# Hybrid encoder trunk on one core: sample attention in a software pipeline, other order of the first tiles and of the last projection, and the merged blocks of the third branch split one block later

## The chip, the cores and the metric

The kernel runs on 1 core of one Trainium2 chip. A core has five engines with one instruction queue each: TensorE (PE, its weight loads PEld), VectorE (DVE), ScalarE (ACT), GpSimd (POOL) and SyncE (SP), which here issues all large DMAs. Each engine executes its queue in order. The metric is device time in microseconds (us), the median of several runs.

## The reference, cut to what matters

One layer on a prompt of 2048 rows and on 8 samples of 16 rows, all with 1024 channels:

```python
h = rms_norm(x, norm_g[l])
(a_x, a_b, a_c, a_z, g_q, g_f, g_i, g_z,
 s_q, s_k, s_v, s_z, m_a, m_b, m_c) = split_cols(h @ w_in[l])
# A: o_a = a_b * conv3(a_c * a_x) * silu(a_z)
# B: o_b = rms_norm(hgrn recurrence(g_q, g_f, g_i)) * silu(g_z)
# C: o_sb = stick-breaking attention(rms_norm(s_q), rms_norm(s_k), s_v) * silu(s_z)
# merged = sigmoid(m_a) * (o_a @ w_branch[0:512]) + sigmoid(m_b) * (o_b @ w_branch[512:1024])
#          + sigmoid(m_c) * (o_c @ w_branch[1024:1536])
# y = x + merged @ w_out
```

Stick-breaking attention of one head, with `z = q @ k.T / 8`: the weight of key j is `sigmoid(z_j)` times the product of `1 - sigmoid(z_i)` over all later visible keys i. The prompt attends to itself, 128 queries at a time. Each of the 8 samples attends with its 16 queries to 1024 cached keys and its own 16. Outputs are y, the conv and recurrence states and the new K and V rows.

## The kernel before, in words

**Tiles and phases.** The 2176 rows form 17 tiles of 128 (tile 0 holds the 8 samples, tiles 1 to 16 the prompt). Phase 1 treats them in three groups (tiles 0 to 4, 5 to 10, 11 to 16), each in chunks of 2 or 3 tiles; phase 2, the merge, in four groups of 5, 4, 4 and 4 tiles (`PGROUPS`, L41).

**Split operands.** Every operand of the big products is split in a high part (ACT copy, L176) and a low part (DVE subtraction, L177): `hh, hl` of the normed rows, `whi, wlo` of the weights, `mh, ml` of the merged rows. A product is three matmuls per 128 rows of contraction: high by high, low by high, high by low.

**Phase 1.** A tile of x is loaded, squared (ACT, L505), scaled by its reciprocal root on POOL (L197) and by `g_bc` on DVE (L510), turned with 8 transposes on PE (L521) and split. Projection jobs follow: `proj_chan` (L587, channels on the partitions, 128x384 or 128x256) and `proj_tok` (L598, tokens on the partitions). Weights come through `wload` (L185, SP) one job ahead. `post_qk` (L682 to 703) norms q and k, turns them (L700) into the tile `kt` (ACT, L702; one buffer) and writes `kt` to DRAM (L703). Gates, conv and recurrence results go to DRAM tensors too.

**Background.** Attention is written as generators that yield costs; `Background` (L58) advances them by a credit that each step of the main work earns. Sample attention runs beside the projections of the second group (about 600 to 1260 us), prompt attention (`attn_pair`, L257 to 328) beside the third group and the merge. The order of instructions on each engine is then fixed by the build, which places each one by its own readiness there.

**Sample attention before** (L344 on). For each sample b and each batch of up to 3 key blocks (`sg` 2, 1, 0): load and turn the key blocks (L405, ACT copy L406), four score matmuls `z` of 32 columns each, one per pair of heads (L412), sigmoids, the scan and the weights `sp` (DVE, L426), three transposes of `sp` (L429, the own keys with 16 columns), copy to `at_` (L436), and then block by block: load `vc` (L444, SP) and four matmuls `pv` (L447) that use 32 columns of the array each.

**Merge** (`merge_jobs`, L1180). For each group, branch x (0 to 2) and pair of blocks dp, `bjob` does for each 128 output channels d: load the gate, 12 matmuls (L1225), multiply with the gate (DVE, L1231 for x = 0, L1233 otherwise), add to `mp` on POOL (L1234) for x > 0, and for x = 2 the split of `mp` into `mh` and `ml` at once. `ojob` (s = 0 to 3) then projects the group's tiles with 256 columns of w_out: 24 matmuls over k = 0 to 7 for each tile (L1247), the sum with x in `yt` (DVE, L1253; one buffer) and its DMA (L1254). The four `ojob`s of a group are written between the first `bjob`s of the next; those of the last group come last.

Of the kernel before, what the change touches and what calls it, by code (L numbers as in the profile page):

```python
# [16 lines left out]
P = 128  # L17
# [81 lines left out]
def trunk(ctx: ExitStack, tc: tile.TileContext, x_prompt, x_sample, cache_conv, state_hgrn, cache_k, cache_v,  # L99
# [72 lines left out]
    nc.sync.dma_start(g_bc, norm_g[0].partition_broadcast(P))  # L172

    def split(hi, lo, src, eng=None):

        nc.scalar.copy(hi, src)  # L176
        (eng or nc.vector).tensor_tensor(lo, src, hi.bitcast(F32), ALU.subtract)  # L177

    def wload(pieces):

        out = []
        for v in pieces:
            a, b = v.shape[1], v.shape[2]
            st = wp.tile([P, a, b], F32, tag="wst", name="wst", bufs=2)
            nc.sync.dma_start(st, v)  # L185
            hi = wp.tile([P, a, b], F32R, tag="whi", name="whi")
            lo = wp.tile([P, a, b], F32R, tag="wlo", name="wlo")
            split(hi, lo, st)
            out.append((hi, lo))
        return out  # L190

    def rstd_of(ssq, n, count):

        v = small.tile([P, n], F32, tag=f"rv{n}", name="rv")
        nc.gpsimd.tensor_scalar(v, ssq, 1.0 / count, EPS, ALU.mult, ALU.add)
        r = small.tile([P, n], F32, tag=f"rr{n}", name="rr")
        nc.gpsimd.tensor_tensor(r, v, mhalf.broadcast_to([P, n]), ALU.pow)  # L197
        return r
# [58 lines left out]
    def attn_pair(m0, m1):  # L257
# [15 lines left out]
        for m in range(m0, m1):  # L273
# [8 lines left out]
            for i in range(nq):  # L282
# [17 lines left out]
                if b0 > 0:  # L300
                    carry[e][i] = at.tile([P, 1], F32, tag="carry", name="carry", bufs=16)
# [42 lines left out]
    def sample_attention():  # L344
# [45 lines left out]
        for b in range(NB):  # L390
            pv = ps_pv()
            carry = one
            vnew = sa.tile([TS, 8, 64], F32, tag="vnew", name="vnew", bufs=1)
            nc.sync.dma_start(vnew, VV[b * TS:(b + 1) * TS])
            for sg in (2, 1, 0):
                nblk = 2 if sg == 2 else 3
                w = nblk * P + (TS if sg == 2 else 0)
                kt = sa.tile([P, 4, 384], F32, tag="kt", name="kt", bufs=2)
                for bi in range(nblk):
                    blk = 3 * sg + bi  # L400
                    kc = sa.tile([P, 512], F32, tag="cst", name="kc", bufs=3)
                    nc.sync.dma_start(kc, cache_k[0, b, blk * P:(blk + 1) * P].rearrange("t h d -> t (h d)"))
                    tp = ps_tp()
                    for h in range(4):
                        nc.tensor.transpose(tp[:, h * P:(h + 1) * P], kc[:, h * P:(h + 1) * P], idf)  # L405
                    nc.scalar.copy(kt[:, :, bi * P:(bi + 1) * P], tp.rearrange("p (h t) -> p h t", h=4))  # L406
                    yield 1.3
                z = ps_z()
                if sg == 2:
                    nc.tensor.matmul(z[:, 256:256 + TS], idb, nmask, start=True, stop=False, skip_group_check=True)  # L410
                for h in range(4):
                    nc.tensor.matmul(z[32 * h:32 * h + 32, :nblk * P], qz[:, h, b], kt[:, h, :nblk * P],  # L412
                                     start=sg != 2, stop=True, skip_group_check=True)
                if sg == 2:
                    for h in range(4):
                        nc.tensor.matmul(z[32 * h:32 * h + 32, 256:256 + TS], qz[:, h, b],
                                         knew[:, h, b * TS:(b + 1) * TS], start=False, stop=True,
                                         skip_group_check=True)
                nc.scalar.activation(sn[:, 384 - w:384], z[:, :w], AF.Sigmoid, scale=-0.125)
                sp = sa.tile([P, 384], F32, tag="sp", name="sp")  # L420
                nc.scalar.activation(sp[:, :w], z[:, :w], AF.Sigmoid, scale=0.125)
                pr = sa.tile([P, 385], F32, tag="pr", name="pr")
                s_in = sn[:, 384 - w:385][:, ::-1]
                nc.vector.tensor_tensor_scan(pr[:, 384 - w:385][:, ::-1], s_in, s_in, carry, ALU.mult, ALU.bypass)
                carry = pr[:, 384 - w:385 - w]
                nc.vector.tensor_tensor(sp[:, :w], sp[:, :w], pr[:, 385 - w:385], ALU.mult)  # L426
                tp = ps_tp()
                for bi in range(nblk):
                    nc.tensor.transpose(tp[:, bi * P:(bi + 1) * P], sp[:, bi * P:(bi + 1) * P], idf)  # L429
                at_ = sa.tile([P, 384], F32, tag="at", name="at_")  # L430
                if sg == 2:
                    nc.tensor.transpose(tp[0:TS, 256:384], sp[:, 256:256 + TS], idf)
                    nc.scalar.copy(at_[:, 0:256], tp[:, 0:256])
                    nc.scalar.copy(at_[0:TS, 256:384], tp[0:TS, 256:384])
                else:
                    nc.scalar.copy(at_, tp[:, :384])  # L436
                yield 2.0
                for bi in range(3):
                    blk = 3 * sg + bi
                    if blk == 8:  # L440
                        vc, n = vnew, TS
                    else:
                        vc, n = sa.tile([P, 8, 64], F32, tag="vst", name="vc", bufs=3), P
                        nc.sync.dma_start(vc, cache_v[0, b, blk * P:(blk + 1) * P])  # L444
                    for h in range(4):
                        c = bi * P + 32 * h
                        nc.tensor.matmul(pv[32 * h:32 * h + 32, 0:P].rearrange("p (e d) -> p e d", e=2),  # L447
                                         at_[0:n, c:c + 32], vc[0:n, 2 * h:2 * h + 2],
                                         start=sg == 2 and bi == 0, stop=sg == 0 and bi == 2, skip_group_check=True)
                    yield 0.6  # L450
            od = sa.tile([P, P], F32, tag="od", name="od", bufs=1)
            nc.scalar.copy(od, pv[:, 0:P])
            for h in range(8):
                nc.sync.dma_start(OCS[b * TS:(b + 1) * TS, h * 64:(h + 1) * 64],
                                  od[h * TS:(h + 1) * TS, 64 * (h % 2):64 * (h % 2) + 64])
            yield 1.0
# [24 lines left out]
    class Prepare:  # L481
# [30 lines left out]
        def turn(self, i, kk):  # L512
# [10 lines left out]
            split(hh[sl], hl[sl], tp.rearrange("p (k t) -> p k t", k=4))  # L523
# [20 lines left out]
        def first_steps(self):  # L544

            n = len(self.tiles)
            for i in range(n):
                self.fetch(i, xp.tile([P, D], F32, tag="xt", name="xt") if i < 2 else
                           g0p.tile([P, D], F32, tag="xt0", name="xt0", bufs=3))
            for f in (self.square, self.scale):  # L550
# [3 lines left out]
            for i in range(n):  # L554
                if i > 2:
                    self.square(i)
                    yield
                    self.scale(i)
                    yield
                for kk in range(0, KB, 4):  # L560
                    self.turn(i, kk)
                    yield
                    if i == 0:
                        (self.scale if kk else self.square)(2)
                self.ready = i

# [74 lines left out]
    lmax = const.tile([P, 4], F32, name="lmax")  # L641
    nc.vector.tensor_copy(lmax, vec[:, 12:16])
    lexp = const.tile([P, 4], F32, name="lexp")
    nc.vector.tensor_tensor(lexp, vec[:, 12:16], lmax, ALU.subtract)
    ebase = const.tile([P, 1], F32, name="ebase")
    nc.vector.memset(ebase, 2.718281828459045)
    nc.gpsimd.tensor_tensor(lexp, ebase.broadcast_to([P, 4]), lexp, ALU.pow)
    lsum = const.tile([P, 4], F32, name="lsum")
    nc.vector.reciprocal(lsum, lexp)
    lsm = const.tile([P, 4], F32, name="lsm")  # L650
    nc.vector.tensor_tensor(lsm, lexp, lsum, ALU.mult)
    lb = const.tile([P, 4], F32, name="lb")
    nc.vector.tensor_tensor(lb, lsm, lsm, ALU.subtract)
    omlb = const.tile([P, 4], F32, name="omlb")
    nc.vector.tensor_scalar(omlb, lb, -1.0, 1.0, ALU.mult, ALU.add)
# [4 lines left out]
    for h in (1, 2, 4, 8, 16, 32, 64):  # L660
        nblk = 64 // h
        mt = g0p.tile([P, 2, 64], F32, tag="mtmp", name="mtmp", bufs=2)
        nc.gpsimd.memset(mt[:, :, :nblk], 1.0)
        for i in range(2):
            m = mt[:, i, :nblk]
            nc.gpsimd.affine_select(m, m, pattern=[[-2 * h, nblk]], base=-h * i, channel_multiplier=1,
                                    compare_op=ALU.is_ge, fill=0.0)
            nc.gpsimd.affine_select(m, m, pattern=[[2 * h, nblk]], base=h + h * i, channel_multiplier=-1,
                                    compare_op=ALU.is_gt, fill=0.0)
        lmask[h] = const.tile([P, 2 * nblk], I32, name=f"lmask{h}")  # L670
        nc.vector.tensor_copy(lmask[h].rearrange("p (i b) -> p i b", i=2), mt[:, :, :nblk])
# [632 lines left out]
```

## Time and profile before

| what | value |
|---|---|
| median of 3 runs | 3031.82 us (3031.12 to 3034.32) |
| the profiled execution's own time | 3036.76 us |
| its span in the trace | 3035.1 us, 51813 instructions |

The span is what the trace covers; 1.7 us of the profiled execution lie around it. Durations and idle times are in us unless ns stands with them. "PE a <- DVE b: 11.0, 21, 2.3" says that PE stood idle 11.0 us in total, 21 times, at most 2.3, ahead of line a until DVE had done line b. In a timeline a row has its start, its duration and, in brackets, the idle time ahead of it and what ended that. PEclk is the clock that TensorE was granted, as a share of full speed. Busy times of single matmuls overlap, since their ends are modelled; the distance of their starts tells their rate.

### The profile page before, as it was taken

The numbers are of one execution on the slowest core, as the hardware profiler recorded it, in microseconds if no ns is written. First come the engines' busy times: TensorE is split into PE (matmuls) and PEld (weight loads), VectorE is DVE, ScalarE is ACT, GpSimd is POOL, SyncE is SP. The second block draws the span as 40 slices with busy tenths as digits, with TensorE's granted clock in tenths as the row PEclk, the third lists the DMA queues.
The fourth block names the chain that finished last, engine by engine and source line by source line (L and its number), as shares of the span: only waits on it lengthen the run. The fifth ranks groups of instructions, "written<-read, shape, count | busy, mean of one in ns | idle before, by whom it ended". The sixth has DMA issues, their size and how long they took to land. (4 is left out here: it accounts for less than half of the span.)

```text
span 3035.1 us, 51813 instructions
## 1 busy us (share of the span) xinstructions
PE 2934.7 (97%) x19609; PEld 2688.3 (89%) x19609; DVE 1759.2 (58%) x3412; ACT 1230.2 (41%) x2571; POOL 454.7 (15%) x861
## 2 busy tenths in 40 slices
PE   7999999999999999999999999999999899899998
PEld 7999999988988888999899998998998788687887
DVE  5345535652434352636635757567577877978753
ACT  4332232243333333224434444444445555555531
POOL 3110000110100000001322111111012412313211
PEclk9999999999999999999999999999999999999999
DMA  5433323455444444323444232323226455555553
GB/s 178 139 109 112 99 90 105 120 161 166 130 126 138 130 131 121 115 78 114 150 152 127 81 122 81 119 66 100 89 87 216 149 164 171 157 184 170 171 160 121
DMA packets 448842, 394.40 MB, mean 130 GB/s; under 512 B 24809, under 2 KB 388674, under 8 KB 448594
## 3 DMA queue, kind: packets, MB, share of 16 engines
q1 hardware_dynamic: 448594, 391.09, 42.3%
q8 instruction: 155, 2.54, 0.4%
q14 instruction: 93, 0.76, 0.1%
HBM read 303.67 MB, written 87.33 MB: 129 GB/s over the span
## 5 line engine op out<-in xcount | busy, mean ns | idle before, releaser
L587 PE MATMUL acc<-hh,whi 128*128 128x384 f32 (+1 forms) x2688 | 937.8, 349 | 0.5 <-ACT hh L176 0.3
L587 PE MATMUL acc<-hl,whi 128*128 128x384 f32 (+1 forms) x2688 | 887.6, 330 | 0.0
L587 PE MATMUL acc<-hh,wlo 128*128 128x384 f32 (+1 forms) x2688 | 887.5, 330 | 0.0
L177 DVE TENSOR_TENSOR wlo<-wst,whi 128x1024 fp32r<-128x1024 f32 x296 | 372.1, 1260 | 435.0 <-ACT whi L176 420.7
L587 PEld LDWEIGHTS acc<-hh,whi 128*128 128x128 f32 x2688 | 508.1, 189 | 37.3 <-issue 31.1
L587 PEld LDWEIGHTS acc<-hl,whi 128*128 128x128 f32 x2688 | 509.2, 189 | 4.9 <-issue 1.0
L587 PEld LDWEIGHTS acc<-hh,wlo 128*128 128x128 f32 x2688 | 507.3, 189 | 0.0
L176 ACT CAST whi<-wst 128x1024 fp32r<-128x1024 f32 x296 | 311.0, 1051 | 364.1 <-PE acc L587 272.4
L598 PE MATMUL acc<-whi,hh 128*128 128x256 f32 x1088 | 317.2, 292 | 7.2 <-DVE gm L986 5.0
L598 PE MATMUL acc<-wlo,hh 128*128 128x256 f32 x1088 | 308.6, 284 | 0.5 <-DVE wlo L177 0.5
L598 PE MATMUL acc<-whi,hl 128*128 128x256 f32 x1088 | 308.6, 284 | 0.0
L298 DVE TENSOR_TENSOR_SCAN pr<-snb,carry 128x513 f32<-128x513 f32 x192 | 259.4, 1352 | 74.3 <-ACT snb L289 73.2
L271 ACT COPY aT<-tp 128x512 f32<-128x512 f32 (+2 forms) x320 | 167.8, 525 | 236.3 <-PE tp L270 233.6
L303 DVE TENSOR_TENSOR sp<-sp,pr 128x512 f32<-128x512 f32 (+2 forms) x320 | 202.0, 631 | 35.1 <-POOL sp L294 13.2
L598 PEld LDWEIGHTS acc<-whi,hh 128*128 128x128 f32 x1088 | 207.2, 190 | 11.7 <-DVE gm L986 5.7
L289 ACT ACTIVATE snb<-z 128x512 f32<-128x512 f32 (+2 forms) x320 | 172.3, 539 | 90.2 <-PE z L286 85.5
L598 PEld LDWEIGHTS acc<-wlo,hh 128*128 128x128 f32 x1088 | 207.4, 191 | 0.7 <-DVE wlo L177 0.7
L598 PEld LDWEIGHTS acc<-whi,hl 128*128 128x128 f32 x1088 | 207.4, 191 | 0.4
L270 PE MATMUL tp<-idf,sp 128*128 128x128 f32 x1088 | 173.1, 275 | 15.8 <-ACT aT L271 15.1
L1225 PE MATMUL acc<-oh,whi 128*128 128x512 f32 (+2 forms) x480 | 179.8, 376 | 8.6 <-DVE gate L1233 7.1
L298 DVE TENSOR_TENSOR_SCAN pr<-snb,one 128x129 f32<-128x129 f32 (+3 forms) x128 | 114.5, 894 | 112.1 <-POOL snb L294 112.0
L291 ACT ACTIVATE sp<-z 128x512 f32<-128x512 f32 (+2 forms) x320 | 171.7, 537 | 16.9 <-DMA OX<-ot 13.0
(301 smaller groups left out, 4773.4 us busy)
## 6 DMA issues: line engine op xcount, KB each, us to landing
wst<-in_w_in_dram SPq DMA_DIRECT2D x216, 512.0 KB, 3.9
wst<-in_w_branch_dram SPq DMA_DIRECT2D x48, 512.0 KB, 4.0
GM<-gm SPq DMA_DIRECT2D x120, 192.0 KB, 2.0
Kt<-KT SPq DMA_DIRECT2D x80, 256.0 KB, 3.1
gate<-GM SPq DMA_DIRECT2D x72, 256.0 KB, 2.7
kc<-in_cache_k_dram SPq DMA_DIRECT2D x64, 256.0 KB, 2.9
vc<-in_cache_v_dram SPq DMA_DIRECT2D x64, 256.0 KB, 2.8
wst<-in_w_out_dram SPq DMA_DIRECT2D x32, 512.0 KB, 4.5
```

The lines of the kernel that those rows point to most:

```text
L176: nc.scalar.copy(hi, src)
L177: (eng or nc.vector).tensor_tensor(lo, src, hi.bitcast(F32), ALU.subtract)
L270: nc.tensor.transpose(tp[:, j * P:(j + 1) * P], sp[:, j * P:(j + 1) * P], idf)
L271: nc.scalar.copy(aT[:, e, 0:nb, i * P:(i + 1) * P], tp[:, :w].rearrange("p (b q) -> p b q", q=P))
L289: nc.scalar.activation(sn[:, 512 - w:512], z[:, :w], AF.Sigmoid, scale=-0.125)
L291: nc.scalar.activation(sp[:, :w], z[:, :w], AF.Sigmoid, scale=0.125)
L298: nc.vector.tensor_tensor_scan(pr[:, 512 - w:513][:, ::-1], s_in, s_in, one if diag else carry[e][i], ALU.mult, ALU.bypass)
L303: nc.vector.tensor_tensor(sp[:, :w], sp[:, :w], pr[:, 513 - w:513], ALU.mult)
L587: nc.tensor.matmul(acc[:, :n], w[0][a][:, k], hT[b][:, k, :n], start=k == 0 and i == 0, stop=k == KB - 1 and i == 2)
L598: nc.tensor.matmul(acc[:, :256], hT[b][:, k, ti * P:(ti + 1) * P], w[k // 4][a][:, k % 4], start=k == 0 and i == 0, stop=k == KB - 1 and i ...
L1225: nc.tensor.matmul(acc[:, :n], w[0][a][:, k, dd * P:(dd + 1) * P], box[x][b][:, k, sl], start=k == 0 and i == 0, stop=k == 3 and i == 2)
```

## The change

What it does, part by part (lines in brackets are of the kernel before):

1. **Start.** The first tile of x is loaded ahead of `g_bc`. Squares and scales of tiles 3 and 4 are held behind the first weight split, the scale of tile 2 behind the split of tile 0 (`tc.issue_after`). The recurrence's bound, the masks and the selectors of the samples (POOL memsets and selects, small DVE copies) are built with the second job.
2. **`post_qk`.** `kt` gets two buffers.
3. **Sample attention** is written as a pipeline over the 24 batches m: keys of m+1, transposes of m, and then the values of m (12 matmuls) directly followed by the scores of m+1. V blocks are loaded three at a time. The own keys are padded with zeros to 128.
4. **Prompt attention.** `carry` has 9 buffers instead of 16.
5. **Merge.** In the third branch the split of a block is written one block later; in the last group it is written at once as before, and there the addition is on DVE. In the first `ojob` of the last group three tiles at a time go through k = 0 to 5 and then through k = 6 and 7. `xr` has 3 buffers (2), `yt` 2 (1).

```diff
 (first_steps)
                 self.fetch(i, xp.tile([P, D], F32, tag="xt", name="xt") if i < 2 else
                            g0p.tile([P, D], F32, tag="xt0", name="xt0", bufs=3))
+                if i == 0:
+                    nc.sync.dma_start(g_bc, norm_g[0].partition_broadcast(P))
...
                 if i > 2:
-                    self.square(i)
-                    yield
-                    self.scale(i)
-                    yield
+                    with tc.issue_after(first_split[0].ins), tc.issue_after(first_split[1].ins):
+                        self.square(i)
+                        yield
+                        self.scale(i)
+                        yield
...
-                    if i == 0:
-                        (self.scale if kk else self.square)(2)
+                    if i == 0 and not kk:
+                        self.square(2)
+                if i == 0:
+                    with tc.issue_after(self.last[1].ins):
+                        self.scale(2)
 (post_qk)
-        kt = qk.tile([P, 4, P], F32R, tag="kt", name="kt", bufs=1)
+        kt = qk.tile([P, 4, P], F32R, tag="kt", name="kt", bufs=2)
 (sample_attention)
+        sps = [single([P, 384], F32, f"sps{i}") for i in range(2)]
+        for x in sps:
+            nc.gpsimd.memset(x, 0.0)
...
+        def turned(m):
...
+            for bi in range(3):
+                nc.tensor.transpose(tp[:, bi * P:(bi + 1) * P], sp[:, bi * P:(bi + 1) * P], idf)
+            at_ = sa.tile([P, 384], F32, tag="at", name="at_")
+            nc.scalar.copy(at_, tp[:, :384])
+            for bi in range(blocks(m)):
+                blk = 3 * sg + bi
+                vc = sa.tile([P, 8, 64], F32, tag="vst", name="vc", bufs=3)
+                nc.sync.dma_start(vc, cache_v[0, b, blk * P:(blk + 1) * P])
...
+        for m in range(last + 1):
+            if m < last:
+                yield from keys(m + 1)
+            turned(m)
+            yield 2.0
+            z = masked(m + 1) if m < last else None
+            values(m)
+            if z is not None:
+                scores(m + 1, z)
+            yield 2.2
 (bjob)
-                            nc.gpsimd.tensor_tensor(m, m, gate[:, sl], ALU.add)
+                            (nc.vector if final and x == 2 else nc.gpsimd).tensor_tensor(
+                                m, m, gate[:, sl], ALU.add)
                         if x == 2:
-                            split(box["h"][:, d, sl], box["l"][:, d, sl], m)
+                            box["due"].append((box["h"][:, d, sl], box["l"][:, d, sl], m))
+                            while len(box["due"]) > (0 if final or d == 7 and chunk is pg[-1] else len(pg)):
+                                split(*box["due"].pop(0))
 (ojob)
+            cuts = [KB - 2, KB] if final and s == 0 else [KB]
...
+                    for c, end in enumerate(cuts):
+                        for ti in some:
...
+                            for k in range(cuts[c - 1] if c else 0, end):
```

The order on PE in the middle of the sample attention, beside a projection with 384 columns (`pv` are the values of one batch, `z` the scores of the next). Before:

```order
L587 MATMUL acc<-hh,wlo 128x384
L447 MATMUL pv<-vc,at__11137 32x128 x4
L587 MATMUL acc<-hh,whi 128x384
L587 MATMUL acc<-hl,whi 128x384
L587 MATMUL acc<-hh,wlo 128x384
L587 MATMUL acc<-hh,whi 128x384
L587 MATMUL acc<-hl,whi 128x384
L587 MATMUL acc<-hh,wlo 128x384
L447 MATMUL pv<-vc,at__11137 32x128 x4
```

Now, with the same projection at L648:

```order
L648 MATMUL acc<-hh,wlo 128x384
L484 MATMUL pv<-vc,at__11236 32x128 x12
L438 MATMUL z<-kt,qz 32x384 x4
L648 MATMUL acc<-hh,whi 128x384
L648 MATMUL acc<-hl,whi 128x384
```

The three groups of four value matmuls stand together, and the scores of the next batch stand right behind them. Over the whole kernel the groups of matmuls on 32 columns that stand apart from each other go from 105 to 33, of which the sample attention has 96 before and 25 now; 8 groups of transposes of 16 columns go as well.

The order on DVE in the third branch of the third merge group, where attention runs beside it (`gate` is the gate product of a block, `ml` the low part of a merged block; `pr` and `sp` belong to attention). Before:

```order
L177 TENSOR_TENSOR ml<-mp,mh 128x512
L303 TENSOR_TENSOR sp<-sp,pr 128x384
L298 SCALAR_TENSOR_TENSOR pr<-snb_15312,one 128x513
L1233 TENSOR_TENSOR gate<-acc,gate 128x512
L303 TENSOR_TENSOR sp<-sp,pr 128x512
L177 TENSOR_TENSOR wlo<-wst,whi 128x1024
L177 TENSOR_TENSOR ml<-mp,mh 128x512
L1233 TENSOR_TENSOR gate<-acc,gate 128x512
```

Now:

```order
L176 TENSOR_TENSOR ml<-mp,mh 128x512
L308 TENSOR_TENSOR sp<-sp,pr 128x384
L303 SCALAR_TENSOR_TENSOR pr<-snb_15278,one 128x513
L1309 TENSOR_TENSOR gate<-acc,gate 128x512
L308 TENSOR_TENSOR sp<-sp,pr 128x512
L176 TENSOR_TENSOR wlo<-wst,whi 128x1024
L176 TENSOR_TENSOR ml<-mp,mh 128x512
L1309 TENSOR_TENSOR gate<-acc,gate 128x512
```

Nothing moved: the same instructions stand in the same order. On ACT, too, the high parts `mh` of this group keep their places. In the second group one `mh` stands three places later, in the first a few pairs are exchanged.

The order on DVE in the third branch of the last merge group, from its first block on (`mp<-mp,gate` is the addition). Before:

```order
L1233 TENSOR_TENSOR gate<-acc,gate 128x512
L177 TENSOR_TENSOR ml<-mp,mh 128x512
L1233 TENSOR_TENSOR gate<-acc,gate 128x512
L177 TENSOR_TENSOR wlo<-wst,whi 128x1024
L177 TENSOR_TENSOR ml<-mp,mh 128x512
L1233 TENSOR_TENSOR gate<-acc,gate 128x512
```

Now:

```order
L1309 TENSOR_TENSOR gate<-acc,gate 128x512
L1310 TENSOR_TENSOR mp<-mp,gate 128x512
L176 TENSOR_TENSOR ml<-mp,mh 128x512
L1309 TENSOR_TENSOR gate<-acc,gate 128x512
L1310 TENSOR_TENSOR mp<-mp,gate 128x512
L176 TENSOR_TENSOR wlo<-wst,whi 128x1024
L176 TENSOR_TENSOR ml<-mp,mh 128x512
L1309 TENSOR_TENSOR gate<-acc,gate 128x512
```

Eight additions of 128x512 came to DVE from POOL; the gates, splits and weight splits keep their order among themselves.

More of the change, by code (lines that the diff above doesn't have):

```diff
@@ L389, in sample_attention @@
         yield 1.0
[L390 to L410, printed above, removed]
-                for h in range(4):
[L412 to L456, printed above, removed]
@@ new lines, in sample_attention, with blocks, keys @@
+        order = [(b, sg) for b in range(NB) for sg in (2, 1, 0)]
+        held = {}
+        pvs = {}
+        sps = [single([P, 384], F32, f"sps{i}") for i in range(2)]
+        for x in sps:
+            nc.gpsimd.memset(x, 0.0)
+        vnew = single([P, 8, 64], F32, "vnew")
+        nc.gpsimd.memset(vnew, 0.0)
+        def blocks(m):
+            return 2 if order[m][1] == 2 else 3
+        def keys(m):
+            b, sg = order[m]
+            kt = sa.tile([P, 4, 384], F32, tag="kt", name="kt", bufs=2)
+            for bi in range(blocks(m)):
+                blk = 3 * sg + bi
+                kc = sa.tile([P, 512], F32, tag="cst", name="kc", bufs=3)
+                nc.sync.dma_start(kc, cache_k[0, b, blk * P:(blk + 1) * P].rearrange("t h d -> t (h d)"))
+                tp = ps_tp()
+                for h in range(4):
+                    nc.tensor.transpose(tp[:, h * P:(h + 1) * P], kc[:, h * P:(h + 1) * P], idf)
+                nc.scalar.copy(kt[:, :, bi * P:(bi + 1) * P], tp.rearrange("p (h t) -> p h t", h=4))
+                yield 1.3
+            held[m] = [kt]
@@ new lines, in masked, with scores @@
+        def masked(m):
+            z = ps_z()
+            if order[m][1] == 2:
+                nc.tensor.matmul(z[:, 256:256 + TS], idb, nmask, start=True, stop=False, skip_group_check=True)
+            return z
+        def scores(m, z):
+            b, sg = order[m]
+            nblk = blocks(m)
+            w = nblk * P + (TS if sg == 2 else 0)
+            kt = held[m][0]
+            for h in range(4):
+                nc.tensor.matmul(z[32 * h:32 * h + 32, :nblk * P], qz[:, h, b], kt[:, h, :nblk * P],
+                                 start=sg != 2, stop=True, skip_group_check=True)
+            if sg == 2:
+                for h in range(4):
+                    nc.tensor.matmul(z[32 * h:32 * h + 32, 256:256 + TS], qz[:, h, b],
+                                     knew[:, h, b * TS:(b + 1) * TS], start=False, stop=True,
+                                     skip_group_check=True)
+            nc.scalar.activation(sn[:, 384 - w:384], z[:, :w], AF.Sigmoid, scale=-0.125)
+            sp = sps[m % 2]
+            nc.scalar.activation(sp[:, :w], z[:, :w], AF.Sigmoid, scale=0.125)
+            pr = sa.tile([P, 385], F32, tag="pr", name="pr")
+            s_in = sn[:, 384 - w:385][:, ::-1]
+            carry = one if sg == 2 else held[m - 1][1]
+            nc.vector.tensor_tensor_scan(pr[:, 384 - w:385][:, ::-1], s_in, s_in, carry, ALU.mult, ALU.bypass)
+            nc.vector.tensor_tensor(sp[:, :w], sp[:, :w], pr[:, 385 - w:385], ALU.mult)
+            held[m] = [sp, pr[:, 384 - w:385 - w]]
@@ new lines, in values @@
+        def values(m):
+            b, sg = order[m]
+            at_, vs = held[m][2:4]
+            if sg == 2:
+                pvs[b] = ps_pv()
+            pv = pvs[b]
+            for bi, vc in enumerate(vs):
+                for h in range(4):
+                    c = bi * P + 32 * h
+                    nc.tensor.matmul(pv[32 * h:32 * h + 32, 0:P].rearrange("p (e d) -> p e d", e=2),
+                                     at_[:, c:c + 32], vc[:, 2 * h:2 * h + 2],
+                                     start=sg == 2 and bi == 0, stop=sg == 0 and bi == 2, skip_group_check=True)
+            if sg == 0:
+                od = sa.tile([P, P], F32, tag="od", name="od", bufs=1)
+                nc.scalar.copy(od, pv[:, 0:P])
+                for h in range(8):
+                    nc.sync.dma_start(OCS[b * TS:(b + 1) * TS, h * 64:(h + 1) * 64],
+                                      od[h * TS:(h + 1) * TS, 64 * (h % 2):64 * (h % 2) + 64])
@@ L457, in sample_attention @@
+        last = len(order) - 1
+        yield from keys(0)
+        scores(0, masked(0))
+        yield 0.7
+        for m in range(last + 1):
[8 more added lines that the diff above has]
+            yield 2.2
         oc = sa.tile([P, 512], F32, tag="cst", name="oc", bufs=3)
```

134 lines of the change are left out of this document (82 added, 52 removed).

## Prediction

> **What bounds the kernel now.** I read the page's busy times and the granted clock first, then the waits of TensorE, since only they can show what the busiest engine loses, then stretches of time with the clock in them, and last the timelines around the places that the change touches.
>
> ```profile
> PE 2934.7 (97%) x19609; PEld 2688.3 (89%) x19609; DVE 1759.2 (58%) x3412; ACT 1230.2 (41%) x2571; POOL 454.7 (15%) x861
> ```
> ```profile
> core 0: 3035.1 us, clock 0.991
> ```
>
> TensorE is busy for 97% of the span, so the bound is TensorE's stream, and a change that leaves the products alone can win three things: the 100 us in which PE is idle (3035.1 - 2934.7), the time that a lowered clock costs ((1 - 0.991) x 3035.1 = 27 us at most), and time that counts as busy but in which the array fills and drains. The waits that this change touches, in the list of PE's waits (total, times, longest):
>
> ```profile
> PE tp L270 <- ACT aT L271: 15.1, 7, 4.6
> ...
> PE tp L429 <- DVE sp L426: 11.0, 21, 2.3
> ...
> PE hg L700 <- ACT kt L702: 7.4, 6, 2.3
> ...
> PE acc L1247 <- ACT mh L176: 5.7, 3, 2.7
> ...
> PE pv L447 <- ACT at__7899 L436: 1.0, 1, 1.0
> ```
>
> The second and the last belong to sample attention, the third to `post_qk`, the fourth to the last merge group, the first to prompt attention beside the third branch. A short wait costs more than itself. In the windows below (length, busy time of PE, PEld, DVE, ACT and POOL, then PEclk, DMA share, GB/s) the clock is below 1.0:
>
> ```profile
> 60.00:80.00 20.00, 17.11 (x125) 16.93 (x125) 8.88 (x22) 5.81 (x13) 3.76 (x6) 0.83 0.58 177
> 660.00:680.00 20.00, 17.65 (x128) 15.18 (x127) 9.13 (x20) 8.09 (x14) 2.96 (x4) 0.91 0.57 163
> 700.00:720.00 20.00, 17.02 (x126) 14.23 (x125) 8.65 (x15) 5.96 (x12) 1.35 (x2) 0.91 0.67 193
> 800.00:820.00 20.00, 17.77 (x132) 16.22 (x131) 6.95 (x14) 6.96 (x16) 2.40 (x4) 0.91 0.44 143
> 1500.00:1520.00 20.00, 15.56 (x102) 14.57 (x101) 12.60 (x22) 7.70 (x18) 3.89 (x8) 0.91 0.69 211
> 1630.00:1650.00 20.00, 18.11 (x138) 17.68 (x139) 4.85 (x12) 6.35 (x16) 2.83 (x8) 0.91 0.48 145
> 2970.00:3000.00 30.00, 22.40 (x137) 20.01 (x136) 12.08 (x17) 6.48 (x8) 6.79 (x4) 0.83 0.37 112
> ```
>
> Each of them holds one of those waits. Of the 1630 window, the wait and the stretch behind it:
>
> ```profile
> 1638.11 0.53 PE L700 MATMUL hg<-idr,st 128*128 128x128 f32 x4 [1.89 <-ACT kt L702]
> ```
> ```profile
> 1639.60:1642.60 3.00, 3.00 (x14) 2.82 (x14) 0.04 (x1) 1.68 (x5) 0.37 (x2) 0.50 0.28 90
> ```
>
> PE waited 1.89 us, and 1.5 us later it ran for 3 us at half clock, though it was busy throughout: 1.5 us lost behind a wait of 1.9.
>
> **The change part by part.** The sum is made against the profiled execution, 3036.76 us with its span of 3035.1, and carried to the median of 3031.82 by subtracting the 4.9 us between them.
>
> *Start.*
>
> ```profile
> 7.90 1.06 POOL L809 MEMSET qblk<- 128x1152 f32 x1
> ```
> ```profile
> 9.53 1.28 DVE L510 SCALAR_TENSOR_TENSOR xt<-xt,rr,g_bc 128x1024 f32<-128x1024 f32 x1 [7.59 <-POOL rr L197]
> ...
> 19.86 1.28 DVE L510 SCALAR_TENSOR_TENSOR xt<-xt,rr,g_bc 128x1024 f32<-128x1024 f32 x1
> ```
>
> The memset stands on POOL ahead of the first tile's root, which releases the first scale; gone, the first transposes come 1.1 us earlier. The scales of tiles 3 and 4 leave DVE's queue ahead of the first weight split: 2 x 1.28 = 2.6. Together 3.6, and I take 3.5. The bounds are 1.0, the memset alone, and 4.9, with a third scale out of the way. Loading x ahead of `g_bc` is in this.
>
> *Two buffers of `kt`.*
>
> ```profile
> 64.39 0.59 ACT L702 CAST kt<-tp 128x512 fp32r<-128x512 f32 x1 [3.18 <-DMA KT<-kt]
> ...
> 68.91 0.59 ACT L702 CAST kt<-tp 128x512 fp32r<-128x512 f32 x1 [2.98 <-DMA KT<-kt]
> ```
> ```profile
> 69.82 0.42 DVE L986 TENSOR_TENSOR gm<-acc,gm 128x256 f32<-128x256 f32 x1 [2.63 <-ACT gm L985]
> ```
> ```profile
> 70.30 0.58 PE L598 MATMUL acc<-whi,hh 128*128 128x256 f32 x1 [2.89 <-DVE gm L986]
> ```
>
> ACT waits for the write of the tile before; behind it in its queue stand the evacuations that PE needs. So PE's 2.89 here is this wait too, under another name. With two buffers a copy waits for the write before last, begun 4.5 us earlier (68.91 - 64.39). Idle: 7.4 + 2.9 = 10.3. Clock, by three windows: 0.17 x 20 + 2 x 0.09 x 20 = 7.0 at most; 6, since part of the slowed time is idle anyway. Of 16.3 I take four fifths, 13, since what releases PE second is not far behind here. Bounds: 5 (half of the idle time, no clock) and 17.
>
> *Sample attention, waits.* Between scores and transposes lie, in the new order, the keys of the next batch with work of the projections, so sigmoids, scan and product are done when PE comes. Idle 11.0 + 1.0 = 12.0; clock by three windows 3 x 0.09 x 20 = 5.4 at most, of which 4.8; four fifths of 16.8 make 13.4. Bounds 8 and 17. Late next would be a key block's or V block's load.
>
> *Sample attention, merged groups.*
>
> ```profile
> 1008.10 0.34 PE L587 MATMUL acc<-hl,whi 128*128 128x384 f32 x1
> ...
> 1008.28 0.34 PE L587 MATMUL acc<-hh,wlo 128*128 128x384 f32 x1
> ...
> 1008.54 0.16 PEld L447 LDWEIGHTS pv<-vc,at__11137 128*32 128x32 f32 x8 [0.25 <-issue]
> 1008.55 0.43 PE L447 MATMUL pv<-vc,at__11137 128*32 128x128 f32 x8
> ...
> 1008.90 0.45 PE L587 MATMUL acc<-hh,whi 128*128 128x384 f32 x1
> ...
> 1009.19 0.34 PE L587 MATMUL acc<-hl,whi 128*128 128x384 f32 x1
> ```
>
> Projections start every 0.175 us. From 1008.28 to 1009.19 are 0.91 us for two of them and one group of four value matmuls: the group costs 0.91 - 0.35 = 0.56. None of this is in the idle time of PE's waits. Directly behind another, a group costs at most its 0.43, at least the 0.16 of its weight loads; it saves 0.13 to 0.40. A projection's row lasts 0.34 where starts are 0.175 apart, so half a row is overlap, and 0.43 would shrink to 0.22; no row shows that for 32 columns, so I take 0.29 for the group and 0.27 saved. Groups saved: 96 - 25 = 71 in sample attention, 8 of 16-column transposes: 79 x 0.27 = 21.3, bounds 10 and 32. No row of before has scores directly behind values, 24 of these places; if they save nothing, the sum loses 24 x 0.27 = 6.5. The Trainium skill ("TensorEngine Tiling (Array Packing)", Key Properties) says that a change of the tiling mode, not of the tile alone, drains the engine; by that rule scores behind values would drain nothing, which no run here shows yet.
>
> Zero memsets of `sps` and `vnew` (a third of `qblk`'s 1.06 each) lie on POOL, 15% busy. Eight ACT copies fewer free no engine that binds.
>
> *Split one block later, first three groups.* By the order, gates, splits and attention stand on DVE and ACT as before, so this costs nothing: 0. The bounds are the 15.1 of the first wait above, if the delay takes effect after all, and 3 lost. Nine buffers of `carry` hold the eight that live.
>
> *Last group.* PE starts a block's matmul every 40/174 = 0.23 us, one of an output tile every 30/255 = 0.118:
>
> ```profile
> 2930.00:2970.00 40.00, 40.00 (x174) 32.38 (x172) 20.50 (x26) 8.93 (x11) 19.92 (x12) 1.00 0.56 174
> 3000.00:3030.00 30.00, 30.00 (x255) 30.00 (x254) 8.17 (x14) 3.15 (x3) 0.00 (x0) 1.00 0.45 143
> ```
> ```profile
> L177 DVE TENSOR_TENSOR wlo<-wst,whi 128x1024 fp32r<-128x1024 f32 x18 | 22.6, 1258 | 3.5 <-ACT whi L176 3.5
> L1233 DVE TENSOR_TENSOR gate<-acc,gate 128x512 f32<-128x512 f32 x16 | 11.0, 687 | 10.8 <-DMA gate<-GM 10.2 <-PE acc L1225 0.6
> ...
> L177 DVE TENSOR_TENSOR ml<-mp,mh 128x512 fp32r<-128x512 f32 x8 | 5.5, 692 | 15.7 <-ACT mh L176 15.7
> ```
> ```profile
> 2974.83 2.14 POOL mp L1234
> 2976.99 0.63 ACT mh L176
> ```
>
> Per block the chain before is gate 0.69, POOL up to 2.14, ACT 0.63, DVE 0.69. With the addition on DVE at 0.69, DVE has gate, addition and low part, 3 x 0.69, and half a weight split, 0.63: 2.70 us against PE's 12 x 0.23 = 2.76, so DVE keeps up, barely. Behind the last block the chain is 2.7 us (3 x 0.69 + 0.63), and PE has three tiles with k = 0 to 5 to do, 54 x 0.118 = 6.4 us. In the window from 2970 PE is idle 30 - 22.40 = 7.6 us, all of it in this stage; the clock costs 0.17 x 30 = 5.1 at most, of which 3.5; against it I set 1.0 of new waits for DVE. Gain 10, bounds 6 and 12.
>
> *`yt`.*
>
> ```profile
> 3031.67 0.42 DVE L1253 TENSOR_TENSOR yt<-acc,xr 128x256 f32<-128x256 f32 x1 [1.98 <-DMA out_dram<-yt]
> ```
>
> The last sum waits for the write before; with two buffers it waits for PE: 0.5 at the very end, 0 to 1.
>
> Sum: 3.5 + 13 + 13.4 + 21.3 + 0 + 10 + 0.5 = 61.7. The profiled execution would take 3036.8 - 61.7 = 2975.1 us, the median 3031.8 - 61.7 = 2970.
>
> **The rivals.**
>
> *The groups save nothing.* PE's own cost of 32-column matmuls is the whole 0.56, drain or not. For it: no row shows a merged group. Against: 0.43 is its longest row, and the weight queue stood idle 0.25 ahead of it. Without the 21.3: 2991.
>
> *Next-late waits.* PE waits of start, `kt`, sample attention and the last group, 40 us of gain, return half with another releaser: 2990. For it: the 2.89 under another name. Against: DVE and ACT have 42% and 59% free.
>
> *The clock stays.* The dips have a cause of their own, and 6 x 0.8 + 4.8 x 0.8 + 3.5 = 12 are not won: 2982. Against it stands that all seven windows hold such a wait, and 1.89 us was followed by half clock. The Trainium skill ("TensorE: Matmul & The Clock Gate", HAM oscillation) wants idle gaps over about 3.4 us for a drop; by that rule these waits could not cause one. The trace, with 1.89, disagrees.
>
> *The delay works.* The third branch no longer holds prompt attention, and the 15.1 go: 2955. Against it is the order.
>
> *V loads hold the queue (slower).* The three loads of a batch stand in SP's queue and wait there for the values before; weights stand behind them.
>
> ```profile
> vc<-in_cache_v_dram SPq DMA_DIRECT2D x64, 256.0 KB, 2.8
> ```
> ```profile
> SPq L444 <- PE pv L447: 141.1, 59, 8.1
> ```
>
> SP waits there 59 times already, up to 8.1 us, without harm to PE. Should PE stand for the landing, 2.8, in each of the 24 batches, and lose 0.9 more by the clock on average, the price is 24 x 3.7 = 89: 2970 + 89 = 3059. It decides from 61.7/24 = 2.6 us per batch on. Against it: the values before are done, in the new order, ahead of the next keys.
>
> **How the numbers follow.** The forecast has 0.60, idle groups 0.13, next-late waits 0.11, the clock 0.05, the delay 0.05, V loads 0.06. The predicted time is 2970. The range from 2951 to 2996 takes in all cases but the V loads and the forecast's own bounds of the groups (10 either way) and some of the waits; outside lie the V loads and about a tenth for bounds that add up. A measurement of this kernel can tell about 0.2%, 6 us, from no change. All cases but the last are faster by more: 0.94; of the last, 0.04 slower and 0.02 within.
>
> **What would show it.** Right: in the list of PE's waits, L429's and L700's successors under 3 us in all; the clock at 1.00 in the windows where `kt` and sample attention stalled; value matmuls at under 0.3 us per further group; the window of the last group with over 28 us of 30 busy; the waits on aT beside the third branch as long as now. Wrong: PE waiting for `vc` or `kc`, groups 0.5 us apart, or new waits on `gate` and `mp` at the end. A time above 2996 or below 2951 would refute the sum.

## The result and the profile after

The changed kernel takes 2949.56 us (median of 4 runs, 2947.67 to 2953.57) against 3031.47 before: 0.973 of the time, 95% interval 0.9713 to 0.9747, or 82 us less where 62 were forecast, and 1.4 us below the range. The profiled execution of it took 2947.67 us, span 2946.0.

Of the page, the busy times, and the granted clock:

```profile
PE 2886.9 (98%) x19609; PEld 2682.6 (91%) x19609; DVE 1763.5 (60%) x3420; ACT 1228.1 (42%) x2563; POOL 437.4 (15%) x856
```
```profile
core 0: 2946.0 us, clock 0.997
```

PE's idle time fell from 100 to 59 us and its busy time by 48 us, with the same 19609 matmuls. So more than half of the gain is in time that counted as busy. Some 17 us of the gain is half clock: PE's slow stretches, in which the granted clock is 0.50, cost 27 us in the trace of before and 10 in this one. PE's longest waits after:

```profile
PE tp L275 <- ACT aT L276: 13.0, 6, 5.0
PE tp L573 <- DVE xt L562: 9.8, 4, 8.1
PE acc L1301 <- DVE gate L1309: 5.4, 6, 1.3
```

The waits of sample attention for `sp` (11.0) and for `kt` (7.4) are gone from the list, as is that of the last group for `mh` (5.7). The one for aT beside the third branch stands.

Where the time went is read by stages. The boundaries are the same instructions in both kernels: the first projection, a projection shortly before sample attention, one shortly behind it, the end of phase 1, and the third branch of the last group. Windows of before (length, PE, PEld, DVE, ACT, POOL, PEclk, DMA share, GB/s):

```profile
0.00:22.56 22.56, 5.82 (x24) 4.62 (x25) 10.58 (x21) 10.90 (x18) 13.93 (x39) 1.00 0.82 260
22.56:609.90 587.34, 579.59 (x4156) 571.08 (x4155) 287.10 (x762) 179.29 (x393) 50.52 (x107) 0.99 0.38 113
609.90:1255.80 645.90, 628.00 (x4650) 569.38 (x4649) 274.28 (x635) 227.59 (x497) 43.68 (x84) 0.99 0.45 135
1255.80:2280.60 1024.80, 1010.39 (x6449) 950.41 (x6448) 623.59 (x1302) 445.50 (x1003) 153.87 (x358) 1.00 0.35 107
2280.60:2950.60 670.00, 637.85 (x3859) 526.15 (x3858) 534.33 (x653) 351.81 (x646) 176.86 (x266) 0.99 0.55 171
2950.60:3035.10 84.50, 73.04 (x481) 66.68 (x480) 29.35 (x43) 15.07 (x18) 15.84 (x9) 0.94 0.41 130
```

The same stages after:

```profile
0.00:17.95 17.95, 6.19 (x25) 4.74 (x26) 8.34 (x17) 9.03 (x15) 4.20 (x15) 1.00 0.87 282
17.95:594.80 576.85, 574.33 (x4153) 566.71 (x4154) 289.48 (x766) 180.90 (x396) 57.68 (x133) 1.00 0.39 117
594.80:1194.40 599.60, 595.82 (x4649) 573.43 (x4648) 273.54 (x634) 225.34 (x489) 43.34 (x84) 1.00 0.47 144
1194.40:2208.90 1014.50, 1005.94 (x6451) 948.22 (x6450) 623.19 (x1303) 446.41 (x1003) 154.83 (x358) 1.00 0.36 109
2208.90:2874.00 665.10, 636.06 (x3858) 525.37 (x3857) 534.32 (x653) 351.25 (x647) 175.10 (x266) 0.99 0.57 172
2874.00:2946.00 72.00, 68.55 (x481) 64.11 (x479) 34.61 (x51) 15.14 (x18) 2.23 (x2) 1.00 0.48 150
```

Gains by stage: start 4.6, first group 10.5, sample attention 46.3, rest of phase 1 10.3, merge of the first three groups 4.9, last group 12.5; together 89.1, the difference of the two spans. The profiled execution of before was a slow one of its kernel (3036.76 against a median of 3031), so the medians differ by 7 us less. In the sample attention stage PE's busy time fell by 32 us at nearly equal matmul counts. Some 3 us of that is half clock (three slow stretches of 3.4 us before, one after); the experiments below show that the rest is what separate groups cost.

The burst that the prediction costed, in the trace of after:

```profile
993.29 0.34 PE L648 MATMUL acc<-hh,wlo 128*128 128x384 f32 x1
...
993.78 0.86 PE L484 MATMUL pv<-vc,at__11388 128*32 128x128 f32 x24
994.46 0.62 PE L438 MATMUL z<-kt,qz 128*32 128x256 f32 x8
994.89 0.23 PE L442 MATMUL z<-knew,qz 128*32 128x16 f32 x8
995.05 0.44 PE L648 MATMUL acc<-hh,whi 128*128 128x384 f32 x1
995.33 0.34 PE L648 MATMUL acc<-hl,whi 128*128 128x384 f32 x1
```

From the first value matmul to the first score are 0.68 us for three groups, 0.23 per group (a row counts each of the 12 matmuls twice). Alone a group had cost 0.56.

### The profile page after: what moved, and what is told of

Read it like the earlier page. It is cut to its first block, busy times and chain, and to the rows that moved or that the text cites. A ratio compares the mean times of both kernels' runs of the same rounds, so it can differ in the third digit from the quotient of the medians.

```text
span 2946.0 us, 51793 instructions
## 1 busy us (share of the span) xinstructions
PE 2886.9 (98%) x19609; PEld 2682.6 (91%) x19609; DVE 1763.5 (60%) x3420; ACT 1228.1 (42%) x2563; POOL 437.4 (15%) x856
## 5 line engine op out<-in xcount | busy, mean ns | idle before, releaser
L648 PE MATMUL acc<-hh,whi 128*128 128x384 f32 (+1 forms) x2688 | 933.2, 347 | 1.3 <-ACT whi L175 0.8
L648 PE MATMUL acc<-hl,whi 128*128 128x384 f32 (+1 forms) x2688 | 886.6, 330 | 0.0
L648 PE MATMUL acc<-hh,wlo 128*128 128x384 f32 (+1 forms) x2688 | 885.6, 329 | 0.3 <-DVE wlo L176 0.3
L648 PEld LDWEIGHTS acc<-hh,whi 128*128 128x128 f32 x2688 | 507.7, 189 | 25.5 <-issue 17.9
L648 PEld LDWEIGHTS acc<-hl,whi 128*128 128x128 f32 x2688 | 508.6, 189 | 5.0 <-issue 1.0
L648 PEld LDWEIGHTS acc<-hh,wlo 128*128 128x128 f32 x2688 | 506.5, 188 | 0.8 <-DVE wlo L176 0.8
L296 ACT ACTIVATE sp<-z 128x512 f32<-128x512 f32 (+2 forms) x320 | 171.7, 537 | 17.1 <-DMA OX<-ot 13.4
```

Of the source, the lines that this page charges most:

```text
L648: nc.tensor.matmul(acc[:, :n], w[0][a][:, k], hT[b][:, k, :n], start=k == 0 and i == 0, stop=k == KB - 1 and i == 2)
```

## The experiments

Theory after the result: every part that the sum named is real, and three of its terms were set too low: the merged groups (0.37 us each, not 0.27), and the waits of `kt` and of sample attention with their clock, which go as a whole. The rivals are the prediction's own sizes, a gain from the delayed split, and a gain that one part owes to another.

**The second `kt` buffer alone.** On the kernel before:

```diff
-        kt = qk.tile([P, 4, P], F32R, tag="kt", name="kt", bufs=1)
+        kt = qk.tile([P, 4, P], F32R, tag="kt", name="kt", bufs=2)
-                    carry[e][i] = at.tile([P, 1], F32, tag="carry", name="carry", bufs=16)
+                    carry[e][i] = at.tile([P, 1], F32, tag="carry", name="carry", bufs=9)
```

> The kernel before with the second kt buffer alone (and carry at 9, which makes room for it). Theory: the waits behind kt and the slow clock that follows them are the whole of what two stages won (10.5 us each in the stages before and after sample attention), so 19 to 22 us faster than before, about 3011, with the clock at 1.00 in the windows 60 to 80, 1500 to 1520 and 1630 to 1650. Rival, the prediction's own haircut: a fifth comes back as something late next and the clock part only partly goes, 13 us, about 3018. Rival without clock: 10 us, with those three slow stretches still there.

Measured 3006.09 against 3028.74 before: 22.7 us, ratio 0.9921 (0.9908 to 0.9935). That is the theory's size, a little above it. (The kernel before ran again beside each set of experiments. Its median was 3028.74 us beside the buffer alone, the pipeline alone, the last group's part and the undelayed split, 3031.52 beside the groups and the addition on POOL, 3032.48 beside the rest.) Its windows from the first projection to sample attention, and through it:

```profile
22.80:600.20 577.40, 575.27 (x4156) 567.61 (x4155) 287.29 (x762) 179.21 (x393) 50.11 (x107) 1.00 0.38 115
600.20:1231.90 631.70, 618.19 (x4620) 560.71 (x4619) 269.45 (x618) 226.07 (x494) 43.48 (x83) 1.00 0.45 136
```

And in the kernel before, the stretch that answers to the second:

```profile
609.90:1250.90 641.00, 623.11 (x4620) 564.52 (x4619) 269.48 (x618) 226.47 (x494) 43.47 (x83) 0.99 0.45 134
```

The first stage takes 577.4 us instead of 587.3, as in the changed kernel, and sample attention 631.7 instead of 641.0, unpipelined as it was; the clock is at 1.00 in both. One of the three slow stretches that the expectation names stayed, at 1488.6 to 1492.0, right behind the one wait that is left of those for `kt` on ACT and `gm` on DVE:

```profile
PE acc L598 <- DVE gm L986: 2.3, 1, 2.3
```

**The pipelined sample attention alone**, the whole new `sample_attention` in the kernel before:

```diff
+            turned(m)
+            yield 2.0
+            z = masked(m + 1) if m < last else None
+            values(m)
+            if z is not None:
+                scores(m + 1, z)
```

> The kernel before with the pipelined sample attention alone. Theory: the stage's gain is its own: 14 us of waits, 3 of clock, 29 of drains between projections and matmuls of 32 columns, together 46, about 2985. Rival: part of it came from the kt buffer, whose waits in this stage (two of 0.5 to 0.8 us) kept ACT behind; then 40, about 2991. Rival, the prediction's size of a group (0.27 us): 36 to 38, about 2994.

2997.24: 31.5 us, ratio 0.9894 (0.9878 to 0.991), less than any of the three expected, so the theory does not hold: the gain is not the stage's own. PE's waits in this kernel say why:

```profile
PE hg L747 <- ACT kt L749: 11.0, 7, 2.4
PE acc L645 <- DVE gm L1033: 6.3, 5, 3.0
```

Before, these were 7.4 and 5.0. With the waits for `sp` gone, PE came to the `kt` waits, which the one buffer still held. In the stage itself PE still stands idle for 10.9 us of 609.7, where the changed kernel has 3.8 of 599.6:

```profile
608.20:1217.90 609.70, 598.79 (x4651) 574.90 (x4649) 273.56 (x635) 224.12 (x489) 43.11 (x84) 0.99 0.47 142
```

**Both together**, the two edits above in the kernel before:

> The kernel before with both the second kt buffer (and carry at 9) and the pipelined sample attention. Alone they won 22.7 and 31.5 us. Theory: they help each other, because in the pipelined sample attention alone PE still waited 11 us for kt, more than the 7 of before; together 60 to 65 us, about 2966. Rival, they add: 54 us, about 2975. Rival, they overlap, since each removes waits of the same stage: under 50, above 2979.

2971.13 against 3032.48: 61.4 us, ratio 0.9795 (0.9782 to 0.9808). Alone they make 54.2, so by the medians they help each other by 7, as the theory has it, but the intervals of the three are some 4 us each, and the traces do not bear it out. Between the same two projections sample attention takes 645.9 us before, 636.6 with the buffer alone, 609.7 with the pipeline alone and 598.9 with both: 9.3 and 36.2 alone, 47.0 together, 1.5 more than their sum. The 7 comes from the kernel before, whose median was 3.7 lower beside those two runs than here; against 3032.48 they would make 61.7. So the second rival is out, and the theory is not told from plain addition, to which the traces are nearer. The stage of sample attention is now that of the changed kernel, with PE idle for 4.5 us of 599:

```profile
599.80:1198.70 598.90, 594.37 (x4651) 571.91 (x4649) 273.71 (x635) 225.32 (x489) 43.38 (x84) 1.00 0.47 144
```

**What a group costs.** The changed kernel again, as the measure:

> The changed kernel itself, as the measure for the next runs on this chip: 2950, within 3 us.

2950.76, ratio 0.9733 (0.9719 to 0.9746). Then with the values in three groups among projections:

```diff
                                      start=sg == 2 and bi == 0, stop=sg == 0 and bi == 2, skip_group_check=True)
+                if bi < 2:
+                    yield 0.6
...
-            values(m)
+            yield from values(m)
...
-            yield 2.2
+            yield 1.0
```

> The changed kernel with the values of a batch in three groups of four matmuls, projections between them, and the scores right behind the last group: 50 more groups of 32 columns among the projections (83 instead of 33). Theory: each return to the projections costs 0.37 us (29.1 us over 79 groups), so 18 us slower than the changed kernel, about 2968. Rival, the prediction's 0.27: 13 us, about 2963. Rival: the cost is in the matmuls of 32 columns themselves and not in the change between forms, 0 to 3 us, about 2951.

2968.46, ratio 0.9788 (0.9774 to 0.9801): 17.7 us more for 50 groups, 0.35 each. And with projections between values and scores:

```diff
             values(m)
+            yield 1.1
             if z is not None:
                 scores(m + 1, z)
-            yield 2.2
+            yield 1.1
```

> The changed kernel with projections between the values of a batch and the scores of the next: 23 more groups (56 instead of 33). Theory, as the Trainium skill has it for a change of tiling mode: scores right behind values pay no second drain, so apart they cost 0.37 us each, 8.5 us, about 2958. Rival: scores behind values drain as well, because weights and outputs change, 0 to 2 us, about 2951.

2958.84, ratio 0.9759 (0.9746 to 0.9773): 8.1 us more for 23 groups, 0.35 each. The stage of sample attention in these three kernels, in the order told:

```profile
595.10:1198.30 603.20, 599.46 (x4675) 576.99 (x4674) 275.42 (x642) 225.82 (x490) 43.39 (x84) 1.00 0.48 144
```
```profile
596.50:1217.00 620.50, 614.66 (x4673) 572.22 (x4672) 276.05 (x642) 225.81 (x490) 42.97 (x84) 1.00 0.47 140
```
```profile
595.80:1207.00 611.20, 605.71 (x4675) 573.47 (x4673) 275.13 (x642) 225.43 (x490) 43.81 (x84) 1.00 0.47 142
```

The second column, PE's busy time, carries most of it: 599, 615, 606, at nearly the same number of matmuls. So each return from 32 columns to the projections costs 0.35 us, and scores right behind values save as much as values behind values, though weights and outputs change. That agrees with the Trainium skill ("TensorEngine Tiling (Array Packing)", Key Properties): only a change of mode drains, and both use 128x32. That the 0.35 us are such a drain no row shows.

**The last group's part alone**, in the kernel before:

```diff
-                            nc.gpsimd.tensor_tensor(m, m, gate[:, sl], ALU.add)
+                            (nc.vector if final and x == 2 else nc.gpsimd).tensor_tensor(
+                                m, m, gate[:, sl], ALU.add)
...
+            cuts = [KB - 2, KB] if final and s == 0 else [KB]
```

> The kernel before with the last merge group's part alone (addition on DVE and cut first projection there, 3 xr and 2 yt buffers, no delay of the split anywhere). Theory: 12 to 13 us, about 3019: the idle 8 us and the clock's 3.6 go, and 0.5 at the end. Rival: 8 to 9, the idle time alone, since the clock's dip came from something else, about 3023.

3019.45: 9.3 us, ratio 0.9966 (0.9954 to 0.9979), so 6 to 14; it lies between the two, which the runs do not part. The traces do. From the third branch of the last group to the end, the five kernels with the old last group take 83.4 to 85.0 us, each at a granted clock of 0.94; this one takes 71.5, as the changed kernel does:

```profile
2945.20:3016.70 71.50, 68.05 (x481) 63.63 (x479) 34.44 (x51) 15.06 (x18) 2.51 (x2) 0.99 0.48 152
```

That is some 12 us, and the clock's dip goes with the waits, as the theory has it. Then its two halves, undone one at a time in the changed kernel. The addition back on POOL:

```diff
-                            (nc.vector if final and x == 2 else nc.gpsimd).tensor_tensor(
+                            nc.gpsimd.tensor_tensor(
```

> The changed kernel with the additions of the last group's third branch on POOL as before; the cut projection stays. Theory: the chain of gate, POOL up to 2.1 us, ACT and DVE paces the last blocks, which PE reaches before they are split, but the three tiles' k = 0 to 5 cover part: 5 us slower than the changed kernel, about 2955, PE idle 4 us in the last group. Rival: the cut hides all of it, 0 to 1 us. Rival: the addition's engine was all of the gain, 10 to 12 us, about 2961.

2953.24, ratio 0.9745 (0.9732 to 0.9759), 2.5 us more by the medians, which the intervals do not part. Its trace does: the last stage takes 77.3 us instead of 72.0, and PE waits in it:

```profile
PE acc L1336 <- DVE gate L1309: 1.4, 2, 1.0
PE acc L1336 <- ACT mh L175: 1.0, 2, 0.8
PE acc L1336 <- DVE ml L176: 0.7, 2, 0.3
PE acc L1301 <- DVE gate L1309: 0.6, 1, 0.6
```

No cut of the first projection:

```diff
-            cuts = [KB - 2, KB] if final and s == 0 else [KB]
+            cuts = [KB]
```

> The changed kernel without the cut of the last group's first projection: its tiles go through k = 0 to 7 one after the other; the addition stays on DVE. Theory: the first tile has k = 0 to 5 in 2.1 us and then waits for the chain of the last block, 2.7 us, so PE idles 1 to 2 us, 2 us slower than the changed kernel, about 2952. Rival: the cut was most of the gain, 6 us or more, about 2957. Rival: DVE's addition alone is enough, no difference.

2952.5, ratio 0.9734 (0.972 to 0.9747), not told from the changed kernel, and one wait in the last group:

```profile
PE acc L1336 <- ACT mh L175: 0.4, 1, 0.4
```

The third of the expectations: with the addition on DVE the cut is worth 0.4 us. With it on POOL the cut, together with the buffers of `xr` and `yt`, still covers more than half: 5.3 of the stage's 12.5 us are lost, not all.

**The start alone**, all of part 1 in the kernel before:

> The kernel before with the start's part alone. Theory: what comes earlier at the start stays earlier to the end, 4.7 us (the first projection at 17.9 instead of 22.6), about 3025 to 3027 beside 3030. Rival: it is given back at the next wait for weights or kt, 0 to 2 us.

3027.48 against 3032.48: 5.0 us, ratio 0.9983 (0.9974 to 0.9992). It is kept to the end: the first projection came 4.5 us earlier (18.04 instead of 22.56).

**No delay of the split**, in the changed kernel:

```diff
-                            while len(box["due"]) > (0 if final or d == 7 and chunk is pg[-1] else len(pg)):
+                            while len(box["due"]) > 0:
```

> The changed kernel with the splits of the third branch written at once in all groups, nothing else changed. Theory, from the order of the engines: no difference, within 1 us of the changed kernel, about 2950, and in the merge of groups one to three the same waits for aT (13 us) and the same clock loss (6 us). Rival: the 4.8 us that this stage won are the delay's, about 2954, and the waits are those of before (32 us idle instead of 29).

2953.52, ratio 0.9747 (0.9732 to 0.9763). The merge of the first three groups, here and in the kernel without the cut, which keeps the delay and differs from the changed kernel only in the order of PE's last projection:

```profile
2210.90:2882.60 671.70, 639.73 (x3858) 527.73 (x3858) 536.00 (x653) 351.53 (x647) 175.34 (x266) 0.98 0.56 171
```
```profile
2209.10:2879.30 670.20, 637.99 (x3859) 527.11 (x3858) 534.42 (x653) 351.31 (x647) 177.71 (x266) 0.99 0.56 171
```

With the delay this stage took 665.1, 666.3 and 670.2 us in three profiles, without it 671.7. The single stage varies by as much as the difference. All traces together say more. From the first matmul of the merge to the third branch of the last group, the six kernels with the delay (and the addition on POOL in these groups) take 655.6 to 660.3 us, mean 657.4; the seven without it 658.7 to 662.3, mean 660.7. So the delay is likely worth some 3 us, although the order of the engines promised nothing. Only one of the seven differs in the delay alone, so this is not shown, and how the delay would do it stays open.

**Additions of the third branch on DVE in all groups**, in the changed kernel:

```diff
-                            (nc.vector if final and x == 2 else nc.gpsimd).tensor_tensor(
+                            (nc.vector if x == 2 else nc.gpsimd).tensor_tensor(
```

> The changed kernel with the additions of the third branch on DVE in all four groups. Theory: the high parts of the first three groups wait on ACT for POOL's additions, and attention's copies behind them hold PE up (13 to 15 us of waits for aT, 6 of clock); an addition of 0.69 instead of 1.3 to 2.1 us on DVE shortens that, and a third of it goes, 6 us, about 2944. Rival: DVE carries attention's scan there and has no room, so that its 32 more additions of 0.4 to 0.7 us make PE wait for sp or gates, 5 to 10 us slower, about 2957.

2936.03, ratio 0.9682 (0.9669 to 0.9696): 14.7 us below the changed kernel's 2950.76 (ratio 0.9733) and the fastest of all. The merge of the first three groups, and what is left of the wait for aT:

```profile
2209.40:2864.20 654.80, 634.36 (x3860) 523.41 (x3859) 532.12 (x685) 352.74 (x647) 134.48 (x234) 0.99 0.57 175
```
```profile
PE tp L275 <- ACT aT L276: 10.2, 5, 6.0
```

PE is idle 20.4 us there instead of 29.0. It gained more than the third of the waits that I expected: of the 8.6 us only 2.8 are this wait, while 5.6 stood under other names (attention's `pv` behind aT 1.7, its `z` behind `sp` 2.6, the gates 1.3). DVE, busy for 532 of the 655 us, had the room.

## Why the prediction was wrong, step by step

The mechanism held in every part but perhaps the delayed split. The sizes failed: 61.7 us stood where 82 were measured, and by the prediction's own words a time below 2951 refutes the sum. Two steps made most of the miss: the price of a group, and counting four fifths of the waits alone.

- *Merged groups, the step "I take 0.29 for the group and 0.27 saved".* The group costs 0.23 behind another, and a separated one 0.35 more: 79 x 0.35 = 27.7 instead of 21.3. The prediction had the right number in hand: its own overlap of half a row gave 0.22. It went a third of the way back to the bare row of 0.43.
- *`kt` and the waits of sample attention, the step "I take four fifths".* Both together, less 27.7 for the groups, won 61.4 - 27.7 = 33.7. The forecast had 13 + 13.4 = 26.4; with the waits counted whole, 16.3 + 16.8 = 33.1. The fifth was set aside for a second releaser that no row named, and little was late next: one wait for `gm`, of 1.4 to 2.4 us in the kernels with the second buffer. That 33.1 comes so near to 33.7 is partly luck, since the shares were off both ways. `kt` alone won 22.7, where 13 stood and 17 was the bound: all 5.0 us under `gm` went where 2.9 were counted (one wait of 2.3 came), and the buffer also made sample attention 9.3 us shorter by the traces, which the sum left out. So 11.0 are left for the waits of sample attention, where 16.8 stood when counted whole, and without the second buffer they won only 31.5 - 27.7 = 3.8.
- *Last group, 10, and `yt`, 0.5.* 9.3 alone by the runs, some 12 by the stage; PE busy 68.55 of 72.0 us there, and idle only behind its last matmul. Of "gate, addition, low part and half a weight split, 2.70 against 2.76" nothing failed. The chain's tail did not need the cut: the last block's `ml` began 2.1 us behind its gate, in DVE's rows of after,

```profile
2899.63 0.68 DVE L1309 TENSOR_TENSOR gate<-acc,gate 128x512 f32<-128x512 f32 x1
2900.35 0.69 DVE L1310 TENSOR_TENSOR mp<-mp,gate 128x512 f32<-128x512 f32 x1
2901.73 0.69 DVE L176 TENSOR_TENSOR ml<-mp,mh 128x512 fp32r<-128x512 f32 x1 [0.69 <-ACT mh L175]
```

  and one tile with k = 0 to 5 takes those 2.1 us (18 x 0.118).
- *Start, 3.5.* 5.0. The first scale came 2.75 us earlier (9.53 before), not 1.1, since with x loaded ahead of `g_bc` its square begins at 4.42 instead of 6.42; the scales moved out of the way gave the other 1.9:

```profile
4.42 1.06 ACT L557 ACTIVATE junk<-xt 128x1024 bf16<-128x1024 f32 x1 [2.35 <-DMA xt<-in_x_sample_dram]
```
```profile
6.78 1.28 DVE L562 SCALAR_TENSOR_TENSOR xt<-xt,rr,g_bc 128x1024 f32<-128x1024 f32 x1 [4.91 <-POOL rr L202]
```

- *Split one block later, 0.* By the traces likely some 3. The order shown is that of the third group, where nothing moved; in the first two groups a few instructions moved, which the sum put at nothing. Whether they are the cause stays open.
- *The rivals.* None came about in the changed kernel. "Next-late waits" did come about where sample attention was changed without `kt`: 17.3 us of waits for `kt` and `gm`, where before had 12.4. It is the second buffer that takes them away.
- *The range.* Each term's bound was given by itself, and the low end took in that of the groups and some of the waits. A tenth was left for bounds that add up, and they did, since the sizes were lowered for one reason, caution, and missed together: 6.4 for the groups, 7.3 for the waits, 1.5 for the start. By the stages the other 5 of the 20 us are 1.5 of the last group and some 3 of the delay.

The parts in medians: 61.4 + 5.0 + 9.3 = 75.7 of 82. The remaining 6 us lie within the intervals of these runs (about 4 us each). With some 12 for the last group and some 3 for the delay, as the stages have it, they would close.

## What to carry to other kernels

On an engine that is 97% busy, look for time inside "busy": count the places where the stream changes between full and narrow tiles, and price one by the distance of starts around it, not by the rows' lengths. Here a wait that a change takes away went nearly whole, so count it whole unless a row names what is late next; waits under other names behind the same blocked copy belong to it. Price edits that touch one stage as a set: their shares can shift between them. A chain through a slow engine (here POOL's addition ahead of a copy that others stand behind) is worth shortening in every group where it stands, not only in the last, if the engine that takes over its work has room.

## What the runs showed of the hardware

A wait's length does not settle whether half clock follows; it only makes it more likely. In the fourteen traces of this case I counted PE's idle stretches of 0.9 us and more (behind the first 25 us, outside of slow stretches) and whether half clock began near them, at the latest 4.5 us behind: 14 of 177 from 0.9 to 1.5 us, 18 of 61 from 1.5 to 2, 32 of 45 from 2 to 3, and 28 of 31 over 3 us. A slow stretch mostly lasted 3.4 us and cost 1.7. The Trainium skill ("TensorE: Matmul & The Clock Gate", HAM oscillation) speaks of gaps over about 3.4 us; here 2 us were often enough. That ten runs of before spread over 9.7 us and five with the second `kt` buffer, taken beside them, over 0.7 would go with it, but no run shows that link.
